# Softmax times V on one core: probabilities stored so that a transpose's weights lie 8 bytes apart instead of 16

## Chip, cores, metric

One core of one Trainium2 chip. The metric is the device time of one execution in microseconds (us).

## The reference

```python
# scores: (8, 12, 1024, 1024) float32, v: (8, 12, 1024, 64) float32
scores_max = np.max(scores, axis=-1, keepdims=True)
attn = np.exp(scores - scores_max)
attn = attn / (np.sum(attn, axis=-1, keepdims=True) + 1e-8)
return np.matmul(attn, v).astype(np.float32)
```

There are 96 heads. The scores are 403 MB and are read once.

## The kernel before

The loop takes four heads a trip, 24 trips. A head's scores lie in SBUF as 128 partitions x 8 rows x 1024 keys (`s_bufs`, one buffer for each of the four heads). ScalarE (ACT) writes exp as float16 for two rows at a time. For each row of 128 queries TensorE (PE) makes eight 128x128 transposes into PSUM, with the probabilities as weights; VectorE (DVE) copies them out to SBUF (`pt`); eight more matmuls take `pt` as weights and stream 65 columns (64 of v and a column of ones, which gives the sum). DVE then divides.

```python
AHEAD = 4; Q = 32; S = 4          # C = SK // P = 8
v_half = sb_pool.tile([P, S, C, D], FP16, name="v_half")
...
def spread_v(k):                  # 16 DVE copies a trip: v to the partitions of its keys
    for s in range(S):
        nc.vector.tensor_copy(
            out=vones_bufs[k][s * Q : (s + 1) * Q, :, 0:D],
            in_=v_half[k * Q : (k + 1) * Q, s],
        )
...
nc.scalar.activation(             # L240: exp, reads runs of 8 floats, writes runs of 256
    out=p_nat[:, g : g + rows, :].rearrange("p r (s v) -> p s r v", s=S),
    in_=s_bufs[k][:, r + g : r + g + rows, :].rearrange(
        "p r (i s c) -> p s (r i) c", s=S, c=C),
    func=EXP,
)
p_row = p_nat[:, r % EB, :].rearrange("p (q c) -> p c q", c=C)   # step 8 elements = 16 bytes
psT = take(psT_bufs)
for c in range(C):
    nc.tensor.transpose(          # L252
        out=psT[:, c * P : (c + 1) * P], in_=p_row[:, c, :], identity=order16[:])
pt = take(pt_bufs)
nc.vector.tensor_copy(out=pt[:], in_=psT[:])                     # L258
...
nc.tensor.matmul(                 # L135, two rows later
    out=st["psO"][:, b, g * M : (g + 1) * M],
    lhsT=pt[:, c * P : (c + 1) * P], rhs=st["vones"][:, c, 0:M],
    start=(c == 0), stop=(c == C - 1))
...
def last(n0):                     # end of a trip, in the last but one:
    load(AHEAD - 2, BH - 2, (4, 4))
    load(AHEAD - 1, BH - 1, (2, 2, 2, 1, 1))
    store(n0, AHEAD - T)
```

Line numbers of the changed kernel are one to three higher: exp is L243 there, transposes L255, the copy out of PSUM L261, the second matmul L136, the spreads L200.

The softmax here doesn't subtract the row's maximum and nothing guards it: scores larger than these inputs give would overflow.

## Time and profile before

| what | value | read from |
|---|---|---|
| time | 1070.54 us, median of 3 | runs |
| span of the profiled execution | 1068.0 us | page, first line |
| busy: PE, DVE, ACT | 745, 776, 736 us | page, part 1 |
| DMA queue's share of 16 engines | 98.8% | page, part 3 |
| one weight load of a transpose, of the second matmul | 153, 106 ns | groups of instructions |
| exp of 2048 elements | 1901 ns | groups of instructions |

The lines behind this are in the prediction. In a line of groups, the two numbers after the first bar are the busy time in us and the mean duration of one in ns; after the second bar stand the engine's idle time just before these instructions and what ended it. In a timeline line the first two numbers are the start and the length (from the start of the first to the end of the last), "xN" counts merged instructions, and a bracket gives the idle time before them. PEld is the weight loads' part of PE. The granted clock is the share of TensorE's full clock that it was given in a stretch; 1.00 is all of it.

### The profile page before, as it was taken

What the parts mean: (1) busy time and instruction counts of PE and PEld (TensorE: products, weight loads), DVE (VectorE), ACT (ScalarE), POOL (GpSimd) and SP (SyncE); (2) the same over time, 40 slices, a digit from 0 to 9 for tenths busy, and PEclk for the clock granted to TensorE, in tenths of its full rate; (3) what the DMA queues carried; (4) which work ended last, traced back from release to release, by engine and by line L of the source; (5) the groups of instructions that cost most, each with busy time, mean ns of one, the idle gap of its engine ahead of it and who ended that gap; (6) DMA issues with size and microseconds to landing.
All of it is one profiled execution on the core that took longest, in us unless ns stands there. A gap on an engine that the chain in (4) does not pass through costs nothing.

```text
span 1068.0 us, 32453 instructions
## 1 busy us (share of the span) xinstructions
PE 745.1 (70%) x12288; PEld 706.6 (66%) x12288; DVE 775.8 (73%) x1517; ACT 736.0 (69%) x432; POOL 48.1 (5%) x31
## 2 busy tenths in 40 slices
PE   3766857767677677775766767667676677775776
PEld 3756757667676577665766757667676576675765
DVE  3675867777677677777676867767777777777677
ACT  3756776666867667586666776666857667686684
POOL 0000000000000000000000000000000000000000
PEclk9887868888698897987878869888788787977889
DMA  9999999999999999999999999999999999999994
GB/s 394 430 424 435 420 444 432 432 432 428 434 432 432 432 432 424 440 432 432 432 430 434 424 440 432 432 432 430 434 432 432 432 432 426 438 432 432 432 424 175
DMA packets 24916, 453.06 MB, mean 424 GB/s; under 512 B 2768, under 2 KB 2768, under 8 KB 9168
## 3 DMA queue, kind: packets, MB, share of 16 engines
q1 hardware_dynamic: 24912, 453.00, 98.8%
q8 instruction: 4, 0.07, 0.0%
HBM read 436.21 MB, written 25.17 MB: 432 GB/s over the span
## 4 chain that ended last, share of the span: by engine, by line
DMA 78%; ACT 12%; PEld 6%; PE 1%; DVE 1%; issue 1%; SPq 0%; ACTq 0%; DVEq 0%; PEldq 0%
DMA s_nat<-in_scores_dram 78%; ACT p_nat L240 12%; PEld L252 4%; PEld L135 2%; DVE pt L258 1%; PE psT L252 1%; PE psO L135 1%; DVE vones L199 0%; SPq L175 0%; DVE out_sb L120 0%; ACTq L240 0%; SPq L187 0%; DVE recip L115 0%; DVEq L221 0%; PEldq L214 0%
## 5 line engine op out<-in xcount | busy, mean ns | idle before, releaser
L240 ACT ACTIVATE p_nat<-s_nat 128x2048 f16<-128x2048 f32 (+1 forms) x408 | 705.2, 1801 | 226.6 <-DMA s_nat<-in_scores_dram 200.7
L252 PE MATMUL psT<-order,p_nat 128*128 128x128 f16 x6144 | 591.4, 252 | 158.5 <-ACT p_nat L240 150.5
L258 DVE COPY pt<-psT 128x1024 f16<-128x1024 f16 x768 | 511.7, 689 | 221.4 <-PE psO L135 97.8
L252 PEld LDWEIGHTS <-p_nat 128*128 128x128 f16 x6144 | 497.4, 153 | 169.8 <-ACT p_nat L240 166.4
L135 PE MATMUL psO<-vones,pt 128*128 128x65 f16 x6144 | 354.3, 204 | 157.8 <-DVE pt L258 117.3
L135 PEld LDWEIGHTS <-pt 128*128 128x128 f16 x6144 | 296.1, 106 | 184.9 <-DVE pt L258 136.6
L120 DVE TENSOR_TENSOR out_sb<-psO,recip 64x512 f32<-64x512 f32 (+1 forms) x240 | 139.7, 582 | 7.8
L199 DVE COPY vones<-v_half 32x512 f16<-32x512 f16 x384 | 109.5, 285 | 23.2 <-POOL v_half L194 6.0
L240 ACT ACT_TABLE_LOAD x24 | 30.8, 1283 | 89.8 <-DMA s_nat<-in_scores_dram 81.7
L194 POOL CAST v_half<-v_sb 128x2048 f16<-128x2048 f32 x25 | 47.4, 1896 | 994.4 <-DMA v_sb<-in_v_dram 658.3
L115 DVE RECIPROCAL recip<-psO 128x8 f32<-128x8 f32 (+1 forms) x120 | 22.8, 190 | 34.0 <-PE psO L135 34.0
L70 DVE MEMSET vones<- 128x16 f16 x4 | 0.2, 72 | 0.8 <-PEq L292 0.8
L61 DVE CAST order<-ident 128x128 f16<-128x128 f32 x1 | 0.2, 226 | 0.4 <-POOL ident masks.py:199 0.4
masks.py:199 POOL TENSOR_SCALAR_AFFINE_SELECT ident<-ident 128x128 f32<-128x128 f32 x1 | 0.3, 294 | 0.1
masks.py:197 POOL MEMSET ident<- 128x128 f32 x1 | 0.2, 205 | 0.3 <-POOLq L292 0.3
L292 POOL MEMSET const-float32-0.0<- 128x1 f32 x1 | 0.1, 99 | 0.2 <-issue 0.2
L292 POOL MEMSET const-bfloat16-1.0<- 128x1 bf16 x1 | 0.1, 103 | 0.0
L292 POOL MEMSET const-uint8-127<- 128x1 uint8 x1 | 0.1, 103 | 0.0
L292 POOL MEMSET const-float32-1.0<- 128x1 f32 x1 | 0.1, 99 | 0.0
## 6 DMA issues: line engine op xcount, KB each, us to landing
s_nat<-in_scores_dram SPq DMA_DIRECT2D x96, 4096.0 KB, 36.0
v_sb<-in_v_dram SPq DMA_DIRECT2D x24, 1024.0 KB, 37.5
out_dram<-out_sb SPq DMA_DIRECT2D x48, 512.0 KB, 27.6
s_nat<-in_scores_dram SPq DMA_DIRECT2D x2, 2048.0 KB, 33.5
s_nat<-in_scores_dram SPq DMA_DIRECT2D x3, 1024.0 KB, 32.6
s_nat<-in_scores_dram SPq DMA_DIRECT2D x2, 512.0 KB
```

The source lines that it names most:

```text
L61: nc.vector.tensor_copy(out=order16[:].rearrange("p (t j) -> p t j", t=T), in_=ident32[:].rearrange("p (j t) -> p t j", t=T),)
L70: nc.vector.memset(vo[:, :, D : D + 2], 1.0)
L115: nc.vector.reciprocal(out=recip, in_=psO[:, :, :, D : D + 1])
L120: nc.vector.tensor_tensor(out=rows.rearrange("j (b g) d -> j b g d", g=G), in0=psO[part, :, :, 0:D], in1=recip[part].to_broadcast([W, last ...
L135: nc.tensor.matmul(out=st["psO"][:, b, g * M : (g + 1) * M], lhsT=pt[:, c * P : (c + 1) * P], rhs=st["vones"][:, c, 0:M], start=(c == 0), ...
L194: nc.gpsimd.tensor_copy(out=v_half[:], in_=v_sb[:])
L199: nc.vector.tensor_copy(out=vones_bufs[k][s * Q : (s + 1) * Q, :, 0:D], in_=v_half[k * Q : (k + 1) * Q, s],)
L240: nc.scalar.activation(out=p_nat[:, g : g + rows, :].rearrange("p r (s v) -> p s r v", s=S), in_=s_bufs[k][:, r + g : r + g + rows, :].rea ...
L252: nc.tensor.transpose(out=psT[:, c * P : (c + 1) * P], in_=p_row[:, c, :], identity=order16[:],)
L258: nc.vector.tensor_copy(out=pt[:], in_=psT[:])
L292: nc = _bacc.Bacc("TRN2", target_bir_lowering=False, num_devices=1)
```

## The change

Its intent (the prediction names the page that it rests on): let each 16-byte line of SBUF serve two elements of a weight load instead of one. Keys are dealt to the transposes in runs of four rather than eight, so exp stores runs of four next to each other and a transpose's weights lie four float16 apart. v's rows are regrouped to match.

```diff
+    L = 4
-    v_sb = sb_pool.tile([P, S, C, D], FP32, name="v_sb")
-    v_half = sb_pool.tile([P, S, C, D], FP16, name="v_half")
+    v_sb = sb_pool.tile([P, C // L, S, L, D], FP32, name="v_sb")
+    v_half = sb_pool.tile([P, C // L, S, L, D], FP16, name="v_half")
 ...
-                out=vones_bufs[k][s * Q : (s + 1) * Q, :, 0:D],
-                in_=v_half[k * Q : (k + 1) * Q, s],
+                out=vones_bufs[k][s * Q : (s + 1) * Q, :, 0:D].rearrange(
+                    "i (h l) d -> i h l d", l=L
+                ),
+                in_=v_half[k * Q : (k + 1) * Q, :, s],
 ...
-                                "p r (s v) -> p s r v", s=S
+                                "p r (x v) -> p x r v", v=Q * L
-                                "p r (i s c) -> p s (r i) c", s=S, c=C
+                                "p r (i x l) -> p x (r i) l", i=Q, l=L
 ...
-                p_row = p_nat[:, r % EB, :].rearrange("p (q c) -> p c q", c=C)
+                p_row = p_nat[:, r % EB, :].rearrange("p (h q l) -> p h l q", q=P, l=L)
-                        in_=p_row[:, c, :],
+                        in_=p_row[:, c // L, c % L, :],
```

(The load of v has its pattern renamed to match; cut.)

More of the change, by code (lines that the diff above doesn't have):

```diff
@@ L187, in load_v @@
             nc.sync.dma_start(
-                out=v_sb[:].rearrange("x s c d -> x (s c d)"),
+                out=v_sb[:].rearrange("x h s l d -> x (h s l d)"),
                 in_=rows[bass.ds(n // AHEAD, 1)].rearrange("o x y -> (o x) y"),
```

## The prediction

> **What bounds the kernel now.** I read the page of the whole execution first, then the groups of instructions, the chain of waits in order of time, and the busy times of single stretches, the end above all. The page's busy times and its transfer rows:
>
> ```profile
> span 1068.0 us, 32453 instructions
> PE 745.1 (70%) x12288; PEld 706.6 (66%) x12288; DVE 775.8 (73%) x1517; ACT 736.0 (69%) x432; POOL 48.1 (5%) x31
> DMA  9999999999999999999999999999999999999994
> q1 hardware_dynamic: 24912, 453.00, 98.8%
> HBM read 436.21 MB, written 25.17 MB: 432 GB/s over the span
> ```
>
> No compute engine is busy for more than 73% of the span, while the transfers' row is at 9 in every slice but the last and the queue's packets fill 98.8% of the 16 DMA engines' time. The chain of waits shows the same thing as a rhythm, one trip of the loop (four heads) at a time:
>
> ```profile
> 878.56 1.92 ACT p_nat L240
> 922.24 1.92 ACT p_nat L240
> 929.79 36.06 DMA s_nat<-in_scores_dram
> 965.95 1.92 ACT p_nat L240
> 973.51 36.02 DMA s_nat<-in_scores_dram
> 1009.64 1.92 ACT p_nat L240
> ```
>
> The first exp of a trip starts every 43.68 to 43.71 us. A trip moves four heads of scores of 4 MiB, 1 MiB of v and 1 MiB of output, 18.87 MB in all. 18.87 MB in 43.69 us is 432 GB/s: the period is the transfer time and nothing else. A 4 MiB load takes 4.194 MB / 432 GB/s = 9.7 us by itself but lands 36.0 us after its issue, so some 26 us of other transfers stand ahead of it in the queue. A shift of a few us in when the engines free a buffer cannot leave the queue empty. Hence 24 trips x 43.69 = 1048.6 us are fixed by bytes, and only the start (about 2 us) and the end are left to the engines. For the end, the stretches (PE, PEld, DVE, ACT, POOL busy, clock, DMA share, GB/s):
>
> ```profile
> 964.00:1008.00 44.00, 31.16 (x522) 29.34 (x518) 33.15 (x65) 30.67 (x18) 1.90 (x1) 0.84 1.02 439
> 1044.00:1052.00 8.00, 7.07 (x136) 6.62 (x134) 6.90 (x12) 7.92 (x6) 0.00 (x0) 1.00 0.74 304
> 1052.00:1060.00 8.00, 5.85 (x109) 5.47 (x108) 7.31 (x14) 0.38 (x1) 0.00 (x0) 1.00 0.16 66
> 1030.19 22.19 ACT L240 ACTIVATE p_nat<-s_nat 128x2048 f16<-128x2048 f32 x13 [1.07 <-DMA s_nat<-in_scores_dram]
> 1039.87 1.41 DVE L120 TENSOR_TENSOR out_sb<-psO,recip 64x512 f32<-64x512 f32 x2
> 1041.31 2.58 DVE L258 COPY pt<-psT 128x1024 f16<-128x1024 f16 x4
> 1062.55 0.88 DVE L120 TENSOR_TENSOR out_sb<-psO,recip 64x256 f32<-64x256 f32 x2
> ```
>
> (The last four are from the timeline.) Scores stop arriving at about 1050 us, ACT ends its last exp at 1052.4, but DVE's last multiply ends at 1063.4 and the store then runs to 1068. In that end DVE is the busiest: 7.31 of 8 us against 5.85 for PE. The reciprocals that close three successive heads start at 1038.80, 1046.69 and 1054.37: 7.7 to 7.9 us a head. DVE's own work makes that up: eight copies, some back to back at 0.645 us (the 2.58 us group of four), some with a 0.27 us pause that comes even where the transposes had ended 0.3 to 0.6 us before, plus 0.20 + 1.41 us to normalise. PE needs only about 0.78 us a row there (a transpose group of eight loads from 1034.33, the next from 1035.11), 6.2 us a head. So PE waits for DVE in the end, and for DMA everywhere else.
>
> **What the Trainium skill says.** (1) "SBUF — State Buffer", Specifications: SBUF has 16-byte lines, at least two hits per line are needed for full bandwidth, and each crossing to a new line costs. Weights 16 bytes apart hit each line once, weights 8 bytes apart twice. The trace agrees with the first half, by the two kinds of weight load in one kernel:
>
> ```profile
> L252 PEld LDWEIGHTS <-p_nat 128*128 128x128 f16 x6144 | 497.4, 153 | 169.8 <-ACT p_nat L240 166.4
> L135 PEld LDWEIGHTS <-pt 128*128 128x128 f16 x6144 | 296.1, 106 | 184.9 <-DVE pt L258 136.6
> L240 ACT ACTIVATE p_nat<-s_nat 128x2048 f16<-128x2048 f32 x360 | 659.6, 1901 | 226.6 <-DMA s_nat<-in_scores_dram 200.7 <-SPq L214 25.5
> L199 DVE COPY vones<-v_half 32x512 f16<-32x512 f16 x384 | 109.5, 285 | 23.2 <-POOL v_half L194 6.0
> ```
>
> Strided by 16 bytes a load takes 153 ns, dense 106; in the timeline at full clock eight take 0.58 against 0.35 us. That 8 bytes is enough, no run here shows yet. (2) "ScalarE: Activation LUTs", What ACT_TABLE_LOAD costs: an ACTIVATE with immediate scale and bias takes 186 ns + 0.833 ns an element, 1892 ns for 2048. The trace has 1901, so reading in runs of 8 with jumps of 128 bytes costs nothing today. (3) "SBUF — State Buffer", A bandwidth-pool intuition that's wrong: DMA to SBUF is listed at 432 GB/s measured. The trace has just that, so there is no room above the present rate.
>
> **The change part by part.** The order of instructions on every engine is unchanged; only shapes differ (exp's output becomes 128x8x2x128 instead of 128x4x2x256).
>
> *Transposes' weights.* 6144 loads, 153 ns to about 106: 47 ns x 6144 = 289 us of summed durations. As busy time, scaled by the same ratio, PEld of that line falls from 497 to 497 x 106/153 = 345 us. The transposes (252 ns, 591 us busy) wait partly on their weights; in the timeline eight take 0.68 us at full clock, and I expect 0.45 to 0.55. All of it lies beside transfers, except in the end. There PE is already ahead of DVE, so I look only for DVE pauses longer than 0.27 us that end on PE: 0.37 before 1032.10, 0.60 before 1033.39, 0.39 before 1052.92, with 0.49 before 1013.89. Their excess is 0.10 + 0.33 + 0.12 + 0.22 = 0.8 us; faster transposes win perhaps half: -0.4 us.
>
> *Exp.* The same 2048 elements, read in runs of 4 floats (16 bytes) instead of 8, written in runs of 128 instead of 256. Every line touched is still used by four elements in a row, so I expect 1901 ns again: 0.
>
> *v, reordered.* The load and the cast are the same bytes. The 384 spreads read two runs of 256 elements instead of one of 512; the output's inner run of 64 is unchanged: 285 ns again, 0. (A slower one counts in the end only: 16 of them, 5.0 us, open the last trip on DVE.)
>
> Sum: 1070.54 - 0.4 = about 1070.1 us.
>
> **The rivals.** *ACT becomes the bound through the shorter runs.* A trip has 15 exps of 1901, two of 1044 and a table load of 1283 ns: 28.5 + 2.1 + 1.3 = 31.9 us of 43.69. To be the bound the exps must grow by (43.69 - 1.3) / 30.6 = 1.39 times, to 2.63 us. One ACT element time (0.83 ns) lost at each of 512 runs makes 2.33 us: still hidden, at most 2 us in the end. Two lost make 2.75 us, a trip of 45.5 us, and 1070 + 24 x 1.8 = about 1113 us. Against it: today's 256 jumps cost at most 9 ns in all.
> *The end was PE's, not DVE's.* The chain of waits does run through PE in many pieces between 1032 and 1060. If each of the last trip's 32 rows gained 0.2 us, 6 us would go: 1064 us. Against it: three heads at DVE's pace of 7.7 us or more, with PE's work only 6.2.
> *Spreads leave a fast copy mode.* At 285 to 550 ns, 16 x 0.27 = 4 us more in the end: 1074 us. DVE has 12 us to spare in a trip, so it stays hidden there.
> *The weights stay slow at 8 bytes.* Nothing changes: 1070.5 us.
>
> **Range and chances.** The three runs before differ by 0.5 us. With 0 to 1 us gained in the end and small changes of ACT or DVE of 1 or 2 us at worst, 1068.5 to 1072 should hold it 8 times in 10. Faster by 2% would need 21 us, more than the whole part of the span that is not transfers (1068 - 1048.6 = 19.4 us): 0.01. Slower by 2% needs an exp of about 2.6 us or more: 0.03. Same: 0.96.
>
> **What would show it.** Right: weight loads of p_nat at 100 to 115 ns, PE's busy time down by about 100 us, the DMA queue still above 98%, the first exps of trips 43.7 us apart, the last multiply within 1 us of 1063.4, exp at 1.90 us and spreads at 285 ns. Wrong: exp above 2.6 us with ACT near 100% busy, idle slices in the transfers' row, or an end in which DVE's pauses shrink with PE's faster rows and the span loses several us.

## The result, and the profile after

Changed kernel: 1070.08 us median of 4 runs (1069.80 to 1071.11). Before, beside it: 1070.75 us median of 4. The ratio is 0.9996, 95% interval 0.9978 to 1.0013: the same, and no gain is shown. Some executions of a program fall into a slower state; all profiled runs quoted were in the fast one, except pv8 and pv4 below: a single run on one core has no known state. (A ratio is the mean time of one kernel's fast runs over that of the other's of the same rounds, so it is not quite the ratio of the medians quoted.)

The page and the groups of the changed kernel:

```profile
PE 713.4 (67%) x12288; PEld 663.8 (62%) x12288; DVE 775.3 (73%) x1517; ACT 735.8 (69%) x432; POOL 48.1 (5%) x31
DMA  9999999999999999999999999999999999999994
q1 hardware_dynamic: 24912, 453.00, 98.8%
...
L243 ACT ACTIVATE p_nat<-s_nat 128x2048 f16<-128x2048 f32 x360 | 659.4, 1901 | 226.5 <-DMA s_nat<-in_scores_dram 200.6 <-SPq L217 25.5
L255 PEld LDWEIGHTS <-p_nat 128*128 128x128 f16 x6144 | 441.2, 123 | 177.4 <-ACT p_nat L243 177.0
L200 DVE COPY vones<-v_half 32x512 f16<-32x512 f16 x384 | 109.4, 285 | 23.2 <-POOL v_half L195 6.0 <-PE L255 3.2 <-DVE out_sb L121 2.7
```

The transposes' weight loads did get shorter, from 153 to 123 ns (497 to 441 us busy), and PE lost 32 us of busy time. Exp and the spreads are what they were. The transfers' row is as full as before. The chain of waits (start, length, what) keeps the rhythm:

```profile
922.24 1.92 ACT p_nat L243
965.92 1.92 ACT p_nat L243
1009.59 1.92 ACT p_nat L243
```

A trip still takes 43.67 to 43.68 us. PE's 32 us came out of time in which it now waits a little longer. The end of the program, from DVE's timeline, with the pauses that the prediction had singled out and the last multiply:

```profile
1032.02 0.69 DVE L261 COPY pt<-psT 128x1024 f16<-128x1024 f16 x1 [0.38 <-PE psO L136]
1033.32 0.69 DVE L261 COPY pt<-psT 128x1024 f16<-128x1024 f16 x1 [0.60 <-PE psO L136]
1038.72 0.20 DVE L116 RECIPROCAL recip<-psO 128x8 f32<-128x8 f32 x1
1046.62 0.20 DVE L116 RECIPROCAL recip<-psO 128x8 f32<-128x8 f32 x1
1052.85 1.53 DVE L261 COPY pt<-psT 128x1024 f16<-128x1024 f16 x2 [0.39 <-PE L136]
1054.30 0.20 DVE L116 RECIPROCAL recip<-psO 128x8 f32<-128x8 f32 x1
1062.47 0.88 DVE L121 TENSOR_TENSOR out_sb<-psO,recip 64x256 f32<-64x256 f32 x2
```

Every time is 0.07 or 0.08 us earlier than before (1038.80, 1046.69, 1054.37, 1062.55), and the pauses are the old ones (0.37, 0.60, 0.39). Nor was this won in the last trip's pauses: the shift was there already at the trip's first copy (1012.63 us, before 1012.71), and its first exp had started 0.05 us sooner (1009.59, before 1009.64).

Why the loads gained less than forecast shows in groups of eight transposes, first of the kernel before, then of the changed one. The first line of each is at a granted clock of 0.50 (the mean from 1030.6 to 1033.4 us, the same in both kernels), the others at 1.00; the changed kernel's next two groups are shown too:

```profile
1031.02 1.04 PE L252 MATMUL psT<-order,p_nat 128*128 128x128 f16 x8
1034.36 0.69 PE L252 MATMUL psT<-order,p_nat 128*128 128x128 f16 x8
```

```profile
1030.94 1.04 PE L255 MATMUL psT<-order,p_nat 128*128 128x128 f16 x8
1034.29 0.61 PE L255 MATMUL psT<-order,p_nat 128*128 128x128 f16 x8
1034.74 0.42 PE L136 MATMUL psO<-vones,pt 128*128 128x65 f16 x8
1034.99 0.61 PE L255 MATMUL psT<-order,p_nat 128*128 128x128 f16 x8
```

At half clock the group takes 1.04 us with weights at either distance: there the load was not what set the pace. At full clock it fell by 0.08 us only. These lengths include the last one's run to its end, so the pace is read better from the starts: (1034.74 - 1034.29) / 8 = 56 ns for a transpose with its 128 columns, (1034.99 - 1034.74) / 8 = 31 ns for a second matmul with its 65. In the kernel before a transpose took 66 ns (the next group started at 1034.89).

### The profile page after: what moved, and what is told of

The parts are those of the page before. It is cut to its first block, busy times and chain, and to the rows that moved or that the text cites. A ratio compares the mean times of both kernels' runs of the same rounds, so it can differ in the third digit from the quotient of the medians.

```text
span 1067.8 us, 32453 instructions
## 1 busy us (share of the span) xinstructions
PE 713.4 (67%) x12288; PEld 663.8 (62%) x12288; DVE 775.3 (73%) x1517; ACT 735.8 (69%) x432; POOL 48.1 (5%) x31
## 3 DMA queue, kind: packets, MB, share of 16 engines
q1 hardware_dynamic: 24912, 453.00, 98.8%
## 4 chain that ended last, share of the span: by engine, by line
DMA 78%; ACT 12%; PEld 4%; PE 2%; DVE 2%; issue 1%; SPq 0%; ACTq 0%; DVEq 0%; PEldq 0%
DMA s_nat<-in_scores_dram 78%; ACT p_nat L243 12%; PEld L255 3%; PEld L136 1%; PE psT L255 1%; DVE pt L261 1%; PE psO L136 1%; DVE vones L200 0%; SPq L176 0%; DVE out_sb L121 0%; ACTq L243 0%; SPq L188 0%; DVE recip L116 0%; DVEq L224 0%; PEldq L217 0%
## 5 line engine op out<-in xcount | busy, mean ns | idle before, releaser
L255 PE MATMUL psT<-order,p_nat 128*128 128x128 f16 x6144 | 550.2, 245 | 165.0 <-ACT p_nat L243 161.6
L255 PEld LDWEIGHTS <-p_nat 128*128 128x128 f16 x6144 | 441.2, 123 | 177.4 <-ACT p_nat L243 177.0
L136 PEld LDWEIGHTS <-pt 128*128 128x128 f16 x6144 | 291.5, 106 | 220.0 <-DVE pt L261 171.3
```

Source lines behind the costliest of these rows:

```text
L136: nc.tensor.matmul(out=st["psO"][:, b, g * M : (g + 1) * M], lhsT=pt[:, c * P : (c + 1) * P], rhs=st["vones"][:, c, 0:M], start=(c == 0), ...
L255: nc.tensor.transpose(out=psT[:, c * P : (c + 1) * P], in_=p_row[:, c // L, c % L, :], identity=order16[:],)
```

## The experiments

My theory: the transfers set the loop, DVE sets the end, and so a faster PE gains nothing; and 8 bytes is already full speed for a load, the rest of the 123 ns being the pace of 128-column transposes. Rivals: PE paces the end; 8 bytes is only half way to dense; the change is worth something that the transfers hide.

**How far apart: 4 and 2 bytes.** The changed kernel with another run length; PE's and DVE's order of instructions is the same as in it (the traces agree).

```diff
-    L = 4
+    L = 2      # l2;  L = 1 in l1
```

> Keys reordered in runs of two: weights 4 bytes apart, exp reads runs of two floats (8 bytes). Theory A (8 bytes already load at full speed; what is left of the 123 ns is set by the 128-column transposes between the loads): weight loads of the transposes stay at 121 to 125 ns mean, eight of them at full clock at 0.48 us. Theory B (the cost of a load falls on with the distance, 8 bytes are half way to dense): mean 110 to 116 ns, eight in about 0.40 us. Exp: if two elements in a 16-byte line are enough for a read, as the skill's page on SBUF says, 1901 ns and the time is within 0.2% of the kernel before (about 1070 us). If the number of runs counts, exp rises above 2000 ns; the time stays within 1% while exp is below 2630 ns.

> No reordering of weights: they are dense (2 bytes apart), and exp reads single floats 128 bytes apart. Theory A: weight loads of the transposes still 121 to 125 ns mean, eight at full clock in 0.48 us. Theory B: 104 to 108 ns like those of pt, eight in 0.35 us. Exp: one element of each 16-byte line is used in turn, so by the same page exp should slow. If it takes less than 2630 ns the time stays at 1070 us with at most 3 us more; if it takes more, ACT becomes the bound, the trip is 1.3 us + 16.1 exps, and for an exp of 3000 ns the time is about 24 x 49.6 + 20 = 1210 us. If exp stays at 1901 ns, the time is 1070 us and the rule of the page is not seen in ACT's reads.

Measured: l2 correct, 1070.10 us, ratio 0.9999 (0.9982 to 1.0015). l1 correct, 1438.09 us, ratio 1.3438 (1.3415 to 1.3460). Exp in the groups of l2, then of l1:

```profile
L243 ACT ACTIVATE p_nat<-s_nat 128x2048 f16<-128x2048 f32 x360 | 684.7, 1976 | 205.8 <-DMA s_nat<-in_scores_dram 183.9 <-SPq L217 21.6
```

```profile
L243 ACT ACTIVATE p_nat<-s_nat 128x2048 f16<-128x2048 f32 x360 | 1293.0, 3701 | 6.2 <-DMA s_nat<-in_scores_dram 5.9
```

With runs of four floats exp costs no more (1901 ns in the changed kernel), with runs of two it costs 75 ns, with single floats 1800 ns. For l2 that is neither of the two numbers expected (1901, above 2000). The runs that exp writes shrink too, from 128 elements to 64 and 32; no run separates the two, so that the reads are the cause is not shown. At 3701 ns ACT is busy for 98% of the span and is the bound, as the prediction's rival had it from 2630 ns on. A trip, from one table load to the next, is 58.9 us, against 1.3 + 16.1 x 3.701 = 60.9 by the formula in the expectation (exps overlap a little). So the rival was real; the change stops two steps short of it.

The weights: eight transposes at full clock take 0.61 us in the changed kernel, in l2 and in l1 alike, and their loads 0.48, 0.45 to 0.47 and 0.45 to 0.46 us. The group no longer gets faster when the weights move closer: something other than the load sets its pace. That it is the 128 streamed columns fits the 56 and 31 ns above, but no run changed the number of columns alone. The mean duration of one load (111 ns in l2, 124 in l1, where the mean clock was 0.72 instead of 0.84) fits the rival's number in l2 and mine in l1; it tells little, because it mixes clocks.

**The load without the transposes' pace.** The second matmul streams 65 columns, so its loads are not held back. In the changed kernel its weights were read at the wrong places, 16 or 8 bytes apart (results wrong, order unchanged).

```diff
-                lhsT=pt[:, c * P : (c + 1) * P],
+                lhsT=pt[:].rearrange("x (h q l) -> x h l q", q=P, l=8)[:, c // 8, c % 8, :],  # pv8; 4 in pv4
```

> Wrong results on purpose: the changed kernel, but the second matmul takes its weights from pt 16 bytes apart. Its moving operand has 65 columns, so its spacing is set by the load. Dense, eight of these loads take 0.35 us at full clock (mean 106 ns). Both theories: about 0.58 us for eight, as the transposes of the kernel before had, mean about 150 ns. PE gains 0.23 us in each of 32 rows of the last trip; if the end is DVE's, the time is within 2 us of 1070.

> Wrong results on purpose: as pv8, but weights of pt 8 bytes apart. Theory A (8 bytes load at full speed): eight in 0.35 us at full clock, mean 106 ns, as dense. Theory B (half way): eight in 0.45 to 0.50 us, mean 118 to 125 ns. Time 1070 us in either case.

Groups of eight such loads at full clock, of the changed kernel (dense), pv4 and pv8:

```profile
1034.68 0.35 PEld L136 LDWEIGHTS <-pt 128*128 128x128 f16 x8
```

```profile
1034.46 0.36 PEld L136 LDWEIGHTS <-pt 128*128 128x128 f16 x8
```

```profile
1035.05 0.58 PEld L136 LDWEIGHTS <-pt 128*128 128x128 f16 x8
```

8 bytes cost 0.01 us a group more than dense, 16 bytes 0.23. The transposes' loads that follow such a group start 0.28 us after its start in the changed kernel, 0.28 in pv4 and 0.47 in pv8. Over the whole run these loads' busy time was 292 us dense, 311 at 8 bytes and 447 at 16. So 8 bytes is full speed but for about an eighth of the 16-byte penalty: (311 - 292) / (447 - 292) = 12%. The mean of one load at 8 bytes, 120 ns, was the number I had given to the rival; by spacing and by busy time it is my theory that holds. (At 16 bytes the mean was 164 ns where about 150 was expected.) The means missed, and they are the weaker measure.

pv8 took 1070.1 us and pv4 1071.0 us (one run each). pv8 made each row of PE 0.2 us longer, 0.91 us, and the closing reciprocals of the last trip came at 1038.82, 1046.77 and 1054.48, within 0.2 us of the changed kernel's. For the trip's second and third head, all at full clock, this is the best evidence that the end did not follow PE: they took 7.95 and 7.71 us against 7.90 and 7.68. The first head is a weaker case: it started 0.5 us sooner in pv8 (first copy at 1029.25, not 1029.76) and lost that again in its rows at a clock of 0.50.

**PE's margin used up.** The kernel before with the second matmul's weights also 16 bytes apart (pv8's edit applied to it; wrong results, order unchanged).

> Wrong results on purpose: the kernel before, with the second matmul's weights 16 bytes apart as well, the order of instructions unchanged. At full clock PE's row was 0.78 us in the kernel before, 0.71 in the changed one and 0.92 with only the second matmul's weights spread; here about 1.0 us, 8.0 us a head against 7.7 of DVE. Theory (the end is paced by DVE at 7.7 us a head as long as PE needs less): 1070.5 to 1072 us, closing reciprocals 7.9 to 8.2 us apart. If the end followed PE's rate all along, 32 rows x 0.22 = 7 us more than the kernel before, 1077 us.

Measured: 1070.91 us, ratio 1.0008 (0.9993 to 1.0023). DVE's closing reciprocals:

```profile
1039.24 0.20 DVE L115 RECIPROCAL recip<-psO 128x8 f32<-128x8 f32 x1
1047.33 0.20 DVE L115 RECIPROCAL recip<-psO 128x8 f32<-128x8 f32 x1
1055.20 0.20 DVE L115 RECIPROCAL recip<-psO 128x8 f32<-128x8 f32 x1
```

PE's rows are 1.0 us apart at full clock (its transposes start at 1035.93, 1036.93 and 1037.92), and the heads close 8.1 and 7.9 us apart instead of 7.9 and 7.7: as expected, PE's rate at full clock begins to matter only here, and by about 1 us in all (the last multiply starts at 1063.54, not 1062.55), not 7. In the times alone this 1 us is not clear of noise.

**More transposes.** In the changed kernel two of eight were done twice (correct results).

```diff
-                for c in range(C):
+                for c in (0, 0, 1, 1, 2, 3, 4, 5, 6, 7):
                     nc.tensor.transpose(
```

> The changed kernel with two of a row's eight transposes done twice: correct results, PE has a quarter more transposes, some 0.15 us a row, 4.9 us in each trip. Theory (PE is off the path in the loop and in the end): 1070 to 1071.5 us. Rival (the end is PE's): the last trip's 32 rows show it, about 1075 us.

Measured: 1073.28 us, ratio 1.0029 (1.0014 to 1.0045). That is between the two numbers and misses both. Most of DVE's pauses in the last trip became 0.39 us, and heads closed 8.64 us apart. But it isn't a clean test: the scheduler put the transposes and second matmuls in another order, as PE's trace shows, and PE's rows at full clock, 0.82 us where nothing held them, were shorter than pv8's 0.91, which cost next to nothing. So the longer heads at full clock were no lack of PE's rate; which handshake of the new order made the pauses of 0.39 us is left open. In the trip's first rows, at a granted clock of 0.50 (1029.5 to 1036 us), it was PE's rate: its rows were 1.51 us apart there, 1.29 in the changed kernel, and DVE's pauses rose to 0.82 us. Doubling an operation is a poor probe where a scheduler places the rest.

**Without the transfer bound.** Both kernels with half of the scores loaded after the first four heads (all rows computed, on old data: wrong).

```diff
-            load(k, (n0 + (AHEAD + k)) % BH, cond=n0 < BH - AHEAD)
+            load(k, (n0 + (AHEAD + k)) % BH, (R // 2,), cond=n0 < BH - AHEAD)
-            load(AHEAD - 2, (n0 + (2 * AHEAD - 2)) % BH)      # and AHEAD - 1 alike
+            load(AHEAD - 2, (n0 + (2 * AHEAD - 2)) % BH, (R // 2,))
-                load(AHEAD - 2, BH - 2, (4, 4));  load(AHEAD - 1, BH - 1, (2, 2, 2, 1, 1))
+                load(AHEAD - 2, BH - 2, (4,));    load(AHEAD - 1, BH - 1, (2, 2))
```

> Wrong results on purpose: the kernel before with half of the scores' bytes (after the first four heads only rows 0 to 3 of the 8 of each partition are loaded; all 8 are computed). A trip moves 8.4 + 1 + 1 MB, about 24 us of transfers at 432 GB/s, so the engines set the time. DVE has 775.8 / 24 = 32.3 us of work in a trip and pauses besides, ACT 31.9 us, PE about 25 to 28 us. Theory (DVE and ACT are next, not PE): a trip of 34 to 38 us, 840 to 930 us in all, DVE or ACT busy above 88%.

> Wrong results on purpose: the changed kernel with the same halved loads. Theory (DVE and ACT bound what transfers no longer do): within 1% of half_before, though the weight loads are faster by 20%. Rival (PE was the next bound, and the change is only hidden by the transfers): faster than half_before by 2% or more, up to 24 x 32 x 0.07 = 54 us.

Measured: 969.79 us before and 969.25 us changed (ratios to the full kernel 0.9064, 0.9050 to 0.9077, and 0.9059, 0.9045 to 0.9073). The busy times of the two, half_before first:

```profile
PE 688.6 (71%) x12288; PEld 656.1 (68%) x12288; DVE 772.6 (80%) x1517; ACT 743.8 (77%) x432; POOL 48.0 (5%) x31
```

```profile
PE 648.4 (67%) x12288; PEld 604.8 (63%) x12288; DVE 772.1 (80%) x1517; ACT 743.7 (77%) x432; POOL 48.0 (5%) x31
```

PE is 40 us less busy, and the time is the same. So the gain is not merely hidden by the transfers: with a third of the queue idle (66.9% busy) the change is still worth nothing. That does not put PE off the path altogether. In a trip of half_after, from 418 to 423.5 us, the granted clock was 0.50; PE's rows were 1.29 us apart there, and DVE stood waiting for them:

```profile
421.02 0.69 DVE L261 COPY pt<-psT 128x1024 f16<-128x1024 f16 x1 [0.60 <-PE psO L136]
```

half_before has the same pauses of 0.60 us in its trip. So PE sets the pace where its clock is halved, and there weights at 8 bytes save nothing against 16 (1.04 us a group with either). The level was missed (840 to 930 us, an engine above 88%): DVE's work of 772 us comes with 124 us of pauses before its copies, 34 before reciprocals and 23 before spreads, which make 953 of half_after's 966 us. I had counted the work and too little of the pauses.

**Taking work from DVE.** The changed kernel, and the kernel before, with the spreads of v on GpSimd.

```diff
-            nc.vector.tensor_copy(
+            nc.gpsimd.tensor_copy(
                 out=vones_bufs[k][s * Q : (s + 1) * Q, ...
```

> The changed kernel with the 16 spreads of v of a trip on GpSimd instead of DVE: DVE loses 5.0 us at the start of the last trip. Theory (the end is DVE's): the last multiply ends 2 to 5 us sooner, unless the second matmul waits for GpSimd's first spreads, 1065 to 1068 us. Rival (the end is PE's or set by the last scores and ACT): within 1 us of 1070.

> The kernel before (weights 16 bytes apart) with the 16 spreads on GpSimd. If the gain of that move is DVE's alone and the weights' distance has no part in it: 1068.3 us within 0.5, as the changed kernel gave with it.

Measured: pool_spread 1068.25 us, ratio 0.9984 (0.9971 to 0.9998); pool_spread8 1068.18 us, ratio 0.9982 (0.9968 to 0.9996), both correct. The two distances of weights give the same time here as well. DVE closes the last trip's third head in pool_spread so:

```profile
1050.05 0.20 DVE L116 RECIPROCAL recip<-psO 128x8 f32<-128x8 f32 x1
1052.31 1.41 DVE L121 TENSOR_TENSOR out_sb<-psO,recip 64x512 f32<-64x512 f32 x2 [2.06 <-DMA out_dram<-out_sb]
```

DVE is 4.2 us ahead of the changed kernel at 1050.05 (1054.30 there), then gives back 2.06 us: the output buffer still waits for the store of the trip before, which stands in the queue behind the last scores. The median is just above the range expected for this reason.

**A version that beats both.** pool_spread, with that store queued ahead of the last two pieces.

```diff
-                load(AHEAD - 1, BH - 1, (2, 2, 2, 1, 1))
-                store(n0, AHEAD - T)
+                load(AHEAD - 1, BH - 1, (2, 2, 2))
+                store(n0, AHEAD - T)
+                load(AHEAD - 1, BH - 1, (1, 1), 6)      # 6: first row
```

> The changed kernel with the spreads on GpSimd, and in the last trip but one the store of the second pair of heads is queued ahead of the last two pieces of scores. In the run with the spreads on GpSimd DVE stood 2.06 us before 1052.31 waiting for that store to leave the output buffer. Theory: the wait goes and the end comes 1.5 to 2 us sooner, 1066.3 us. If the last scores, 1.2 us later, decide, no gain: 1068 to 1069 us.

Measured: correct, 1065.65 us (0.6 us below the 1066.3 expected), ratio 0.9961 (0.9947 to 0.9975): faster than the kernel before by 0.4%, which the interval holds clear of 1, though by the measure of 2% it counts as the same.

```profile
1050.30 1.41 DVE L121 TENSOR_TENSOR out_sb<-psO,recip 64x512 f32<-64x512 f32 x2
1058.24 0.88 DVE L121 TENSOR_TENSOR out_sb<-psO,recip 64x256 f32<-64x256 f32 x2
```

The wait is gone, and the last multiply starts 4.2 us before the changed kernel's (1062.47). The same end that 32 us less of PE left alone moved by these 4 us when DVE was relieved and its wait for the store taken away.

## Why the prediction was right, point by point

- *Transfers fix the loop.* Right: the trip is 43.67 to 43.68 us and the queue 98.8% busy, and with half of the scores' bytes the time fell to 970 us. Even there the change made no difference.
- *The end is DVE's.* Right where the clock is full: pv8's slower PE rows cost under 0.1 us a head there, both16 marks where PE's rate starts to count (about 1 us a row), and pool_store gains its 4 us by relieving DVE and moving the store. "There PE is already ahead of DVE" was wrong for the rows at a clock of 0.50, where DVE waited for PE (0.37 and 0.60 us, in the changed kernel 0.38 and 0.60). Before its last reciprocal DVE also stands 1.42 us for the second matmuls, whose weights the change doesn't touch.
- *The weights' saving.* The direction was right, the term mis-sized. I put 106 ns and 345 us for the transposes' loads, and 0.45 to 0.55 us for eight transposes at full clock; measured were 123 ns, 441 us and 0.61 us. PE's busy time fell by 32 us, not about 100. The load itself is as fast as I thought (0.36 against 0.35 us in pv4). What I left out is the transpose's own pace, which takes over once the load is faster (56 ns each, most likely its 128 columns): 0.61 us a group with weights 8, 4 or 2 bytes apart, and 1.04 us, before and after, where the granted clock was 0.50.
- *0.4 us from DVE's pauses.* Too much: the pauses kept their length, and the 0.08 us by which all ended sooner came before them. The pauses before 1032 and 1033 lie where the clock was 0.50, so the transposes there were no faster. Why the pause of 0.39 us stayed as well is not settled. That the median came within 0.1 us of the 1070.1 forecast is luck: the kernel before ran between 1069.5 and 1071.1 us.
- *Exp and spreads cost nothing more.* Right: 1901 and 285 ns, as before. The rival needed exp above 2630 ns, which L = 4 doesn't give and L = 1 does.

## What to carry to other kernels

Before making an operation faster, ask what paces its engine once it is: here the transpose's own pace took over after about a third of the forecast saving in load time (56 of 152 us), and where the engine was on the path, at half clock, the load was not what held it. Where transfers set the loop, look for time in the start and the end, and find the engine that paces the end by slowing its neighbour. An access pattern that speeds one engine's read can be paid for in another's work, and here there is a cliff: at single floats exp takes twice as long.

## What the Trainium skill lacked or had wrong

- "SBUF — State Buffer", Specifications: two hits on a 16-byte line are said to give full bandwidth. For weight loads that holds closely (eight loads 0.35 us dense, 0.36 at 8 bytes, 0.58 at 16 bytes). Exp with two floats a line cost 4% (1976 ns against 1901), with one float 95% (3701 ns), its shorter writes included. The page gives no size for the penalty.
- "TensorE: Matmul & The Clock Gate", LDWEIGHTS: 128 columns / 1.2, so 107 ns, is given with no word of the distance of weights, and the page's part on faster weight loads allows strides without giving their cost. At a granted clock of 1.00 the median load of the second matmul lasted 98 ns dense, 115 ns at 8 bytes (pv4) and 171 ns at 16 (pv8); the dense ones' mean over the run, clocks mixed, was 106 ns. Loads overlap: eight dense ones took 0.35 us, not 8 x 98 ns.
- The same page, Part 4, says that the full clock does not engage for transposes. Here groups of eight took 0.61 us at a granted clock of 1.00 and 1.04 us at 0.50, so they do run at it; ordinary matmuls ran between them, and no run shows transposes alone.
